# Second-norm operands stored by token parity, and DRAM weight sums paused while the decay rows load

## The chip, the cores and the metric

The kernel runs on one core of one Trainium2 chip. The metric is the time of one execution on the device, in microseconds. Before the change the median of three runs is 727.8 us (727.13 to 728.92). Engines are named as in the profile: PE is TensorE (its weight loads are shown apart, as PEld), DVE is VectorE, ACT is ScalarE, POOL is GpSimd, and SP is SyncE, which only issues DMAs here. A line such as L864 is a line of the kernel before the change.

## The reference

One layer of a decoder trunk on 512 tokens of width 1024, all in float32: a norm, one wide projection, two token mixers side by side (a block-sparse attention and a chunkwise mLSTM), their gated merge, an output projection with residual, a second norm, a SwiGLU feed-forward of width 2816 with residual, and a final norm.

```python
u = rms_norm(h, norm_mix_g)
z = u @ w_in                       # q/k/v | mLSTM q,k,v,o | gates
A = moba_attention(rope(q), rope(k), v)          # 8 heads x 64
B = mlstm_chunkwise(silu(conv(qk)), v, i, f)     # 4 heads x 128, per-row decay exp(b_t - b_s + i_s - m_t)
h = h + (sigmoid(ga) * (A @ w_proj_a) + sigmoid(gb) * (B_gated @ w_proj_b)) @ w_out
u = rms_norm(h, norm_ffn_g)
g, up = split(u @ w_gate_up)
h = h + (silu(g) * up) @ w_down
return rms_norm(h, norm_final_g)
```

## The kernel before, in words

**Products.** Every float32 product is made of three matmuls: the operands are split into a high and a low half (type fp32r), and high x high, high x low and low x high are summed in PSUM. `split_hl` (L164 to L169) makes the halves: ACT copies the high half, DVE subtracts it to give the low half.

**First stage, the units.** The projections are 60 units (`UNITS`, L53 to L71), each with one 512 KB block of weights and, in most, 24 matmuls of 128x512. `fill` (L376 to L394) runs the next unit `u`: it splits weights up to two units ahead, calls `make_sums` (L387), issues the unit's matmuls, and between these and the unit's evacuation runs a function `mid` that it is given. Weight blocks are loaded in pairs on SP's queue (L193) into nine rotating buffers (`NR`, tag R); a load is issued when a buffer is free.

**The mixer loop** (L1724 to L1763) runs steps `n`; each step from the second on runs one unit, and step n runs unit n + 9. Steps 0 to 15 are the attention's halves of heads, later steps are the mLSTM's. `mid` also starts side work that is listed by step in `todo` (L1720): `ml_w(h)` at steps 13, 16, 17 and 19. `ml_w` calls `ml_load` (L1604), which loads the decay rows of one mLSTM head, tile `R`, from a small DRAM array `scr`, broadcast to 128 partitions: one 896 KB DMA on POOL's queue. Then DVE (L1618) and ACT turn the rows into weights that multiply the mLSTM's scores. The tile comes from the pool of eight 4x512 tiles (tag A4), so the load also waits until such a tile is free.

**Sums in DRAM.** The feed-forward uses a Strassen-like scheme with seven products in place of eight, on halves of tokens and of widths. It needs sums of weight blocks. Some are made in DRAM ahead of time: `sum_steps` (L726) yields 40 steps, alternately a copy of one block to a DRAM tile `ws` (SP's queue, L730) and the addition of the other block (POOL's queue, an accumulating DMA, L732). The blocks have 1 MB (gate and up weights, `wgc`) or 512 KB (down weights, `wds`). `make_sums(n)` (L746) issues steps until n are made, and ties each to the newest matmul of the program so far, so that a step waits in its queue until PE is there ("paced"). `fill` asks for `6 * (u - 17) // 7` steps: the first at unit 19, then six in seven units. In the feed-forward each of the seven products of an item issues one more step (L855).

**Second norm's operands.** `run_wo` (L669 to L704) adds the output projection to the residual, feature block by feature block (`h`, 128 features x 512 tokens), and forms the scheme's seven left operands: `a` and `b` are the first and second 256 tokens of `h`; they are scaled by the norm's gain (L684, L685, L693, L694), combined by further DVE operations, split, and stored in tiles `bq` (`bpair`, `bop`). All of it is elementwise along the tokens.

**Feed-forward.** `ITEMS` (L85) lists the order: five items `gc` (512 columns of gate and up each) interleaved with four items `ds` (the matching rows of the down projection), then two items `gu` (the last 256 columns), then the last `ds`. In `gc_run` (L848) the tokens are the matmul's stationary side: for each product, `q = slice(t, HS, 2)` (L859) takes every second of the 256 tokens of a `bq` operand as a 128x128 stationary tile (t = 0 even, t = 1 odd tokens), and the 512 weight columns move. That makes 5 items x 7 products x 2 x 2 x 2 x 3 = 840 matmuls at L864 to L866. The outputs for t are transposed on DVE (L907) into a tile `ht` in which t is the innermost index, so token order is restored there. In `gu` items (`prod`, L1021) the weights are stationary and the `bq` operand moves, all 256 tokens; `gu_last` (L1075) applies the norm's row `rb2`, SiLU and the product, and splits the result `u` into `h` and `l` (L1093, L1094), which the last `ds` uses as stationary tiles by token. In `ds` the stationary tiles are contiguous (L1107 to L1109).

The order of the feed-forward's instructions comes from `plan` and `at` (L772 to L797), a table of due times by which the scheduler sorts each engine's queue.

Of the kernel before, what the change touches and what calls it, by code (L numbers as in the profile page):

```python
# [12 lines left out]
ALU = mybir.AluOpType  # L13
# [78 lines left out]
def hybrid_layer_kernel(ctx: ExitStack, tc, xT, wall, wgc, wgu, wds, wdl, g3v, vecs, wgates, consts, rope, out):  # L92
# [283 lines left out]
    def fill(n=1, mid=None):  # L376

        for _ in range(n):
            u = pos[0]
            if u >= len(UNITS):  # L380
                if mid:
                    mid()
                return
            while wstate["split"] <= min(u + LOOK, NGEN - 1):
                split_unit()
            pos[0] += 1
            make_sums(6 * (u - 17) // 7)  # L387
            kind, i = UNITS[u]
            g = run[kind](i, *whl.pop(u))
            next(g, None)  # L390
            if mid:
                mid()
            for _ in g:
                pass  # L394
# [7 lines left out]
        mm3(ps, wh, wl, range(8), uh, ul, True, True)  # L402
        return ps

    st = {"made": 0}

    def run_qk(kind):
        def fn(i, wh, wl):
# [241 lines left out]

    trq = []

    def residual():

        while trq:
            n, h = trq.pop(0)
            if n % 4 == 0:
                st["ht"] = slot4(name="ht").rearrange("p j (b e) -> p j b e", e=P)
            o = st["ht"].rearrange("p j b (n e) -> p (j b) n e", e=32)
            V.transpose(o[:, :, n % 4, :], h.rearrange("p (b e) -> p b e", e=32))  # L660
            if n % 4 == 3:
                c = 32 * (n - 3)
                for a in range(4):
                    nc.gpsimd.dma_start(
                        h1d[:, :, 256 * a + c : 256 * a + c + P].rearrange("t (b i) c -> i t b c", i=32),
                        st["ht"][32 * a : 32 * a + 32],
                    )

    def run_wo(i, wh, wl):  # L669
        if len(xr) < KT:  # L670
            load_xr()
        ps = mmb()
        mm3(ps, wh, wl, range(8), [t[0] for t in mgd], [t[1] for t in mgd], True, True)
        residual()
        yield
        m = i
        h = xr[WO.index(m)]
        V.tensor_tensor(h, ps, h, op=ALU.add)
        trq.append((WO.index(m), h))
        a, b = h[:, 0:HS], h[:, HS:S]  # L680
        g, ng = col(G2 + m), ng2[:, m : m + 1]
        if m < 4:
            u = ut[m] = slot(name="ut")
            V.tensor_scalar(u[:, 0:HS], a, g, None, op0=ALU.mult)  # L684
            V.scalar_tensor_tensor(u[:, HS:S], b, ng, u[:, 0:HS], op0=ALU.mult, op1=ALU.add)  # L685
            hh, ll = bpair(0, m)
            act_(hh, u, AF.Copy, scale=-1.0)
            V.scalar_tensor_tensor(ll, u, -1.0, f(hh), op0=ALU.mult, op1=ALU.subtract)
        else:
            k = m - 4  # L690
            u = ut.pop(k)
            v = slot(name="v1")
            V.tensor_scalar(v[:, 0:HS], a, g, None, op0=ALU.mult)  # L693
            V.tensor_scalar(v[:, HS:S], b, ng, None, op0=ALU.mult)  # L694
            split_hl(v, dst=bpair(1, k))
            w = slot(name="v2")
            V.tensor_tensor(w[:, 0:HS], u[:, HS:S], v[:, HS:S], op=ALU.subtract)
            V.tensor_tensor(w[:, HS:S], u[:, 0:HS], w[:, 0:HS], op=ALU.subtract)
            split_hl(w, dst=bpair(2, k))
            V.tensor_tensor(u[:, 0:HS], v[:, 0:HS], w[:, 0:HS], op=ALU.subtract)  # L700
            if k == 0:
                bq[(3, 0)] = slot4(F32R, "bq")
            split_hl(u[:, 0:HS], dst=bop(6, k))
        add_sq(2, h, WO.index(m))  # L704
# [41 lines left out]
    def make_sums(n):  # L746

        while st["made"] < n:
            st["made"] += 1
            i = next(making, None)  # L750
            if i is not None:
                tc.add_manual_dep(raw_ins(i), raw_ins(st["mm"]).name, after, reason="paced")
# [95 lines left out]
    def gc_run(c):  # L848

        key = ("gc", c)  # L850
        g = sw.pop(key)
        two = range(2)

        def product(ps, w, o, first=False):
            make_sums(st["made"] + 1)  # L855
            for j, (wh, wl) in enumerate(g[w]):
                for t in two:
                    at(key, w, 2720 * j + 1360 * t)
                    q = slice(t, HS, 2)  # L859
                    for e in range(2):  # L860
                        k = 2 * j + e
                        bh, bl = (b[:, q] for b in bop(o, k))
                        d = slice(e * S, (e + 1) * S)
                        st["mm"] = T.matmul(ps[t], bh, wh[:, d], start=first and k == 0, stop=False, skip_group_check=not first)  # L864
                        T.matmul(ps[t], bh, wl[:, d], start=False, stop=False, skip_group_check=not first)  # L865
                        T.matmul(ps[t], bl, wh[:, d], start=False, stop=k == 3, skip_group_check=not first)  # L866

        def done(w, t):
            at(key, w, 4080 + 1360 * t)

        def copies(ps, w, name):
            r = []
            for t in two:
                done(w, t)
                r.append(slot(name=name))
                act_(r[t], ps[t], AF.Copy)
            return r

        X = [mmb() for _ in two]
        product(X, "W11", 0, first=True)  # L880
        a = copies(X, "W11", "ga")
        Z = [sb() for _ in two]
        product(Z, "S1", 1, first=True)
        x3 = copies(Z, "S1", "gx")
        product(X, "S2", 4)
        b = copies(X, "S2", "gb")
        yield
        if c == 0:
            second_norm(key)
        rg = st["rg"]  # L890
        Y = [accb() for _ in two]
        product(Y, "W12", 2, first=True)
        for t in two:
            done("W12", t)
            V.tensor_tensor(a[t], Y[t], a[t], op=ALU.subtract)
        yield
        product(X, "S3", 5)
        for t in two:
            done("S3", t)
            V.tensor_tensor(x3[t], X[t], x3[t], op=ALU.add)  # L900
            act_(x3[t], x3[t], AF.Silu, scale=rg[:, t + 2 : t + 3])
        yield
        ht = slot4(name="ht").rearrange("p j (b h e x) -> p (j b) h e x", h=2, e=32, x=2)

        def turn(t, u, s):
            V.tensor_tensor(u, u, s, op=ALU.mult)
            V.transpose(ht[:, :, t // 2, :, t % 2], u.rearrange("p (b e) -> p b e", e=32))  # L907

        product(Z, "S4", 3)
        for t in two:  # L910
            done("S4", t)
            V.tensor_tensor(b[t], Z[t], b[t], op=ALU.add)
            at(key, "W22", 1360 * t)
            turn(t + 2, b[t], x3[t])
        product(X, "W22", 6)
        for t in two:
            done("W22", t)
            s = slot(name="gs")
            act_(s, X[t], AF.Silu, scale=rg[:, t : t + 1])
            turn(t, a[t], s)  # L920
        at(key, "W22", 5440 + 3000)
        d = hid_t[c] = dram.tile([P, 4, S], F32, name=nm("ad"))
        for i in range(4):
            nc.sync.dma_start(
                d[:, i].rearrange("(g o) x -> o g x", o=32), ht[32 * i : 32 * i + 32].rearrange("p (g b) h e x -> p g (b h e x)", g=4)
            )
# [148 lines left out]
    def gu_last(i):  # L1075
        key = ("gu", i)
        g = sw.pop(key)
        x, z, t, u, s12 = g["X"], g["Z"], g["t"], g["u"], g["s"]
        rb2 = st["rb2"]
        at(key, "S4")  # L1080
        prod(z, g["S4"], 3)
        at(key, "W22", E_OFF)
        V.scalar_tensor_tensor(u[:, B_], z, -1.0, s12[:, B_], op0=ALU.mult, op1=ALU.subtract)
        V.tensor_tensor(t[:, B_], t[:, B_], rb2[:, B_], op=ALU.mult)
        at(key, "W22")
        prod(x, g["W22"], 6)
        at(key, "W22", E_OFF + 1500)
        V.tensor_tensor(t[:, A_], x, rb2[:, A_], op=ALU.mult)
        act_(t, t, AF.Silu)
        V.tensor_tensor(u[:, A_], u[:, A_], t[:, A_], op=ALU.mult)  # L1090
        V.scalar_tensor_tensor(u[:, B_], u[:, B_], -1.0, t[:, B_], op0=ALU.mult, op1=ALU.mult)
        h, l = slot(F32R, "ach"), slot(F32R, "acl")
        c = act_(h, u, AF.Copy)  # L1093
        V.tensor_tensor(l, u, f(h), op=ALU.subtract)  # L1094
        hid.append((h, l))
        if i == FT - 1:
            ph["ins"].append(raw_ins(c))
# [626 lines left out]
    while n < len(steps) or qa or qb:  # L1724
# [14 lines left out]
        def mid():  # L1739
# [4 lines left out]
            advance(2 if n < 13 else 3)  # L1744
            second()

        if n:
            fill(1, mid)
        else:
            mid()  # L1750
# [126 lines left out]
```

## Time and profile before

| what | value |
|---|---|
| runs | 727.13, 727.8, 728.92 us; median 727.8 us |
| profiled execution, its own time | 727.12 us |
| its span, first to last instruction | 725.3 us |
| PE granted clock | 0.998 |
| busiest engines | PE 712.7 us, DVE 602.4 us, ACT 429.6 us, POOL 69.9 us |
| DMA | 152.70 MB, 211 GB/s on the mean |

The profile's page gives busy times by engine, the span in 40 slices, the DMA queues, the chain of work that ended last, and groups of instructions by source line. Its views of the trace give the same by stretches of time (windows), by instruction in order of time (timeline), by wait, and by tile. A timeline row has the start, the duration, the engine and line, the operation, out<-in, and in brackets the idle time before it with what ended it. A matmul's duration (0.39 us) is longer than the distance to the next matmul's start, since matmuls overlap in the array: what a matmul costs a busy PE is the distance from start to start.

### The profile page before, as it was taken

Reading aid. Unit: us, or ns where it says so; the run is one execution under the profiler, and the core shown is the slowest. Engines: PE = TensorE matmul, PEld = TensorE weight load, DVE = VectorE, ACT = ScalarE, POOL = GpSimd, SP = SyncE. Lnnn points to the kernel's source line nnn. Section 1 sums busy time; section 2 is a strip of 40 time slices with the busy share of each in tenths; the row PEclk is TensorE's granted clock in tenths of the full one; section 3 lists DMA queues with packets and bytes.
Section 4 is the critical chain, followed back from the end, with each engine's and each line's share of the span. In section 5 each row is a group of like instructions: output and inputs, shape, how many; then the busy total and the mean of one; then the engine's idle time right before and its main releaser. Section 6 shows DMA issues by size and latency. Waiting matters only on the chain.

```text
span 725.3 us, 9566 instructions
## 1 busy us (share of the span) xinstructions
PE 712.7 (98%) x3318; PEld 592.9 (82%) x3318; DVE 602.4 (83%) x982; ACT 429.6 (59%) x706; POOL 69.9 (10%) x97
## 2 busy tenths in 40 slices
PE   9999999999998999999999999999999999999995
PEld 6888788888887888888888888888888888888974
DVE  6799877898968588666699869898999789798996
ACT  7535777668754346723344746566665665575654
POOL 0013010001000000000020110021002004003000
PEclk9999999999999999999999999999999999999999
DMA  9668683676486456978889956479469649869703
GB/s 329 278 212 240 190 239 126 204 214 212 132 278 163 144 172 179 279 253 228 233 260 232 270 189 224 182 197 303 167 203 268 211 131 221 303 156 273 207 1 117
DMA packets 47008, 152.70 MB, mean 211 GB/s; under 512 B 5852, under 2 KB 6244, under 8 KB 42480
## 3 DMA queue, kind: packets, MB, share of 16 engines
q1 hardware_dynamic: 36880, 117.39, 47.3%
q0 software_dynamic: 9792, 34.14, 22.9%
q8 instruction: 26, 0.43, 0.2%
q10 hardware_dynamic: 288, 0.56, 0.2%
q14 instruction: 22, 0.18, 0.1%
HBM read 130.01 MB, written 53.52 MB: 253 GB/s over the span
## 4 chain that ended last, share of the span: by engine, by line
PE 91%; DVE 5%; DMA 2%; ACT 1%; issue 1%; ACTq 0%; DVEq 0%
PE mm L208 12%; PE mm L210 12%; PE mm L209 12%; PE mm L864 5%; PE mm L865 5%; PE mm L866 5%; PE s L864 3%; PE s L865 3%; PE s L866 3%; PE mm L1109 2%; PE mm L1108 2%; PE mm L1107 2%; PE acc L1587 2%; PE mm L491 2%; PE mm L308 2%; PE mm L493 2%
## 5 line engine op out<-in xcount | busy, mean ns | idle before, releaser
L155 ACT ACTIVATE w<-raw 128x1024 fp32r<-128x1024 f32 (+2 forms) x107 | 108.0, 1022 | 52.0 <-PE mm L865 16.2
L155 ACT ACTIVATE wh<-raw 128x1024 fp32r<-128x1024 f32 x56 | 59.1, 1056 | 74.6 <-PE mm L209 72.4
L839 DVE TENSOR_TENSOR w<-raw,w 128x1024 fp32r<-128x1024 f32 x70 | 84.1, 1220 | 18.4 <-ACT w L155 18.3
L168 DVE TENSOR_TENSOR wl<-raw,wh 128x1024 fp32r<-128x1024 f32 x56 | 68.2, 1219 | 9.2 <-ACT wh L155 8.9
L864 PE MATMUL mm<-w,bq 128*128 128x512 f32 x160 | 63.1, 394 | 0.0
L866 PE MATMUL mm<-w,bq 128*128 128x512 f32 x160 | 63.1, 394 | 0.0
L865 PE MATMUL mm<-w,bq 128*128 128x512 f32 x160 | 63.1, 394 | 0.0
L208 PE MATMUL mm<-u,wh 128*128 128x512 f32 x128 | 50.7, 396 | 2.7 <-DVE ga L587 2.5
L210 PE MATMUL mm<-u,wh 128*128 128x512 f32 x128 | 50.1, 391 | 0.0
L209 PE MATMUL mm<-u,wl 128*128 128x512 f32 x128 | 49.9, 390 | 0.0
L210 PE MATMUL mm<-ul,wh 128*128 128x512 f32 x128 | 49.8, 389 | 0.0
L208 PE MATMUL mm<-uh,wh 128*128 128x512 f32 x128 | 49.8, 389 | 0.0
L209 PE MATMUL mm<-uh,wl 128*128 128x512 f32 x128 | 49.8, 389 | 0.0
L864 PEld LDWEIGHTS mm<-w,bq 128*128 128x128 f32 x160 | 30.9, 193 | 6.5
L866 PEld LDWEIGHTS mm<-w,bq 128*128 128x128 f32 x160 | 30.9, 193 | 6.4
L865 PEld LDWEIGHTS mm<-w,bq 128*128 128x128 f32 x160 | 30.9, 193 | 6.4
L1019 DVE TENSOR_TENSOR w<-raw,w 128x1024 fp32r<-128x1024 f32 x25 | 30.2, 1219 | 2.7 <-ACT w L155 1.7
L864 PE MATMUL s<-w,bq 128*128 128x512 f32 x80 | 31.5, 394 | 0.0
L865 PE MATMUL s<-w,bq 128*128 128x512 f32 x80 | 31.5, 394 | 0.0
L866 PE MATMUL s<-w,bq 128*128 128x512 f32 x80 | 31.5, 394 | 0.0
L1107 PE MATMUL mm<-w,ac 128*128 128x512 f32 x80 | 31.4, 392 | 0.0
L1109 PE MATMUL mm<-w,ac 128*128 128x512 f32 x80 | 31.2, 390 | 0.0
(439 smaller groups left out, 1945.5 us busy)
## 6 DMA issues: line engine op xcount, KB each, us to landing
raw<-in_wall_dram SPq DMA_DIRECT2D x56, 512.0 KB, 5.7
raw<-in_wgc_dram SPq DMA_DIRECT2D x30, 512.0 KB, 6.0
raw<-ws SPq DMA_DIRECT2D x30, 512.0 KB, 5.7
ws<-in_wgc_dram SPq DMA_DIRECT2D x10, 1024.0 KB, 6.0
ws<-in_wgc_dram POOLq DMA_DIRECT2D x10, 1024.0 KB, 8.3
raw<-in_wds_dram SPq DMA_DIRECT2D x15, 512.0 KB, 6.1
ws<-in_wds_dram SPq DMA_DIRECT2D x10, 512.0 KB, 4.8
ws<-in_wds_dram POOLq DMA_DIRECT2D x10, 512.0 KB, 6.6
```

Source lines behind the costliest of these rows:

```text
L155: return A.activation(out_, in_, func, **kw)
L168: V.tensor_tensor(l, src, f(h), op=ALU.subtract)
L208: st["mm"] = T.matmul(ps, wh[:, c], rh[j], start=start and j == 0, stop=False)
L209: T.matmul(ps, wl[:, c], rh[j], start=False, stop=False)
L210: T.matmul(ps, wh[:, c], rl[j], start=False, stop=stop and j == n - 1)
L839: V.tensor_tensor(l, t, f(h), op=ALU.subtract)
L864: st["mm"] = T.matmul(ps[t], bh, wh[:, d], start=first and k == 0, stop=False, skip_group_check=not first)
L865: T.matmul(ps[t], bh, wl[:, d], start=False, stop=False, skip_group_check=not first)
L866: T.matmul(ps[t], bl, wh[:, d], start=False, stop=k == 3, skip_group_check=not first)
L1019: V.tensor_tensor(w[k][1], g[k], f(w[k][0]), op=ALU.subtract)
L1107: T.matmul(ps, bh, wh[:, d], start=first and k == 0, stop=False, skip_group_check=not first)
L1109: T.matmul(ps, bl, wh[:, d], start=False, stop=k == 1, skip_group_check=not first)
```

## The change

In four places:

- `gc_run` takes contiguous stationary tiles, `slice(t * P, (t + 1) * P)`. For that, `run_wo` stores the tokens of each operand half by parity: the even ones first, then the odd ones. It reads `h` through a view with stride two (`by_parity`) and writes through a view that is contiguous (`halves`).
- In `gu_last` the 256 tokens of each half are then in parity order too: the norm's row `rb2` is read with stride two, and the result's halves `h` and `l` are written with stride two, back in token order.
- `fill` asks for no new sum steps while `st["hold"]` is set, and otherwise for at most two more at a unit, up to the same schedule as before.
- The mixer loop sets `st["hold"]` in steps 12 to 20, that is for units 21 to 29.

```diff
@@ fill
-            make_sums(6 * (u - 17) // 7)
+            make_sums(st["made"] if st["hold"] else min(st["made"] + 2, 6 * (u - 17) // 7))
...
-    st = {"made": 0}
+    st = {"made": 0, "hold": False}
...
+    def by_parity(t):
+        return t.rearrange("p (j x) -> p x j", x=2)
+
+    def halves(t):
+        return (t[:, c].rearrange("p (x j) -> p x j", x=2) for c in (slice(0, HS), slice(HS, S)))
+
@@ run_wo
-        a, b = h[:, 0:HS], h[:, HS:S]
+        a, b = (by_parity(h[:, c]) for c in (slice(0, HS), slice(HS, S)))
         g, ng = col(G2 + m), ng2[:, m : m + 1]
         if m < 4:
             u = ut[m] = slot(name="ut")
-            V.tensor_scalar(u[:, 0:HS], a, g, None, op0=ALU.mult)
-            V.scalar_tensor_tensor(u[:, HS:S], b, ng, u[:, 0:HS], op0=ALU.mult, op1=ALU.add)
+            lo, hi = halves(u)
+            V.tensor_scalar(lo, a, g, None, op0=ALU.mult)
+            V.scalar_tensor_tensor(hi, b, ng, lo, op0=ALU.mult, op1=ALU.add)
...
             v = slot(name="v1")
-            V.tensor_scalar(v[:, 0:HS], a, g, None, op0=ALU.mult)
-            V.tensor_scalar(v[:, HS:S], b, ng, None, op0=ALU.mult)
+            lo, hi = halves(v)
+            V.tensor_scalar(lo, a, g, None, op0=ALU.mult)
+            V.tensor_scalar(hi, b, ng, None, op0=ALU.mult)
             split_hl(v, dst=bpair(1, k))
@@ gc_run
-                    q = slice(t, HS, 2)
+                    q = slice(t * P, (t + 1) * P)
@@ gu_last
-        V.tensor_tensor(t[:, B_], t[:, B_], rb2[:, B_], op=ALU.mult)
+        lo, hi = halves(t)
+        V.tensor_tensor(hi, hi, by_parity(rb2[:, B_]), op=ALU.mult)
...
-        V.tensor_tensor(t[:, A_], x, rb2[:, A_], op=ALU.mult)
+        V.tensor_tensor(lo, x.rearrange("p (x j) -> p x j", x=2), by_parity(rb2[:, A_]), op=ALU.mult)
...
         h, l = slot(F32R, "ach"), slot(F32R, "acl")
-        c = act_(h, u, AF.Copy)
-        V.tensor_tensor(l, u, f(h), op=ALU.subtract)
+        w, u = (lambda t: t.rearrange("p (s j x) -> p s x j", s=2, x=2)), u.rearrange("p (s x j) -> p s x j", s=2, x=2)
+        c = act_(w(h), u, AF.Copy)
+        V.tensor_tensor(w(l), u, w(f(h)), op=ALU.subtract)
@@ the mixer loop
+        st["hold"] = 12 <= n <= 20
         if n:
             fill(1, mid)
```

## The prediction

> **What bounds the kernel now.** I read the page first, for the share of each engine and for the chain of work that ended last.
>
> ```profile
> PE 712.7 (98%) x3318; PEld 592.9 (82%) x3318; DVE 602.4 (83%) x982; ACT 429.6 (59%) x706; POOL 69.9 (10%) x97
> PEclk9999999999999999999999999999999999999999
> PE 91%; DVE 5%; DMA 2%; ACT 1%; issue 1%; ACTq 0%; DVEq 0%
> ```
>
> PE is busy nearly all the time at full clock, and 91% of the chain is PE. So time is gained where a matmul costs PE less, or where PE stands still. Next the windows, to see where it does and how busy the others are there.
>
> ```profile
> 220.00:240.00 20.00, 17.52 (x86) 14.62 (x85) 14.85 (x25) 9.64 (x16) 0.83 (x1) 1.00 0.61 158
> 380.00:400.00 20.00, 20.00 (x89) 16.57 (x88) 19.07 (x33) 10.04 (x16) 0.83 (x1) 1.00 0.92 233
> 540.00:560.00 20.00, 20.00 (x88) 16.58 (x87) 19.65 (x20) 11.73 (x15) 6.94 (x8) 1.00 1.06 272
> 680.00:700.00 20.00, 19.48 (x108) 16.03 (x106) 19.08 (x30) 12.79 (x19) 0.00 (x0) 1.00 0.21 67
> ```
>
> The columns are PE, PEld, DVE, ACT, POOL, clock, DMA share and GB/s. The first row holds a hole of 2.5 us in PE. At 380 (output projection) and 540 (feed-forward) PE has no hole, though DVE is at 19.1 and 19.7 of 20. At 680 PE has small holes and DVE is full.
>
> **Contiguous stationary tiles.** The cost of a matmul is the distance of starts. These rows of PE's timeline are the first matmul of a unit of the output projection, the first of the first `gc` product 24 matmuls later, and the first of its second product, again 24 later; then the last matmul of a `gc` item and, 24 apart, two of the `ds` stage behind it, where the stationary tile is contiguous and weight columns move as in `gc`.
>
> ```profile
> 386.90 0.39 PE L208 MATMUL mm<-mgh,wh 128*128 128x512 f32 x1
> 392.34 0.39 PE L864 MATMUL mm<-w,bq 128*128 128x512 f32 x1
> 397.94 0.40 PE L864 MATMUL s<-w,bq 128*128 128x512 f32 x1
> ...
> 471.05 0.40 PE L866 MATMUL mm<-w,bq 128*128 128x512 f32 x1
> 471.28 0.39 PE L1107 MATMUL mm<-w,ac 128*128 128x512 f32 x1
> 476.73 0.39 PE L1107 MATMUL mm<-w,ac 128*128 128x512 f32 x1
> ```
>
> The output projection takes 5.44 us for 24, 226.7 ns each; `gc` 5.60, 233.3 ns; `ds` 5.45, 227.1 ns. The groups of weight loads show where it arises:
>
> ```profile
> L864 PEld LDWEIGHTS mm<-w,bq 128*128 128x128 f32 x160 | 30.9, 193 | 6.5
> L1107 PEld LDWEIGHTS mm<-w,ac 128*128 128x128 f32 x80 | 15.0, 188 | 3.6 <-DVE h L1191 0.4 <-issue 0.2
> ```
>
> A load with stride two takes 193 ns, a contiguous one 188. Type, size and moving operand are alike in both; the stride is the only difference that I find. The 840 matmuls of `gc` should fall from 233.3 to between 226.7 and 227.1 ns: 5.2 to 5.6 us, taken as 5.5. PE has no hole in `gc` to absorb it, if DVE keeps up: the full DVE at 540 did so, and 24 matmuls only bring a due time 0.16 us nearer.
>
> [...]
>
> **DVE and ACT with stride two.** In the output projection 12 DVE operations of 128x256 (L684, L685, L693, L694, four each) get a strided input. No row shows a strided read. The nearest is a strided write: L907 writes every second word of `ht`, L660 runs of 32.
>
> ```profile
> L907 DVE STREAM_TRANSPOSE ht<-ga 128x512 f32<-128x512 f32 x10 | 6.6, 690 | 0.0
> L660 DVE STREAM_TRANSPOSE ht<-xr 128x512 f32<-128x512 f32 x8 | 5.6, 703 | 0.0
> L168 DVE TENSOR_TENSOR bq<-v,bq 128x512 fp32r<-128x512 f32 x8 | 5.5, 684 | 0.0
> L168 DVE TENSOR_TENSOR bq<-ut,bq 128x256 fp32r<-128x256 f32 x4 | 1.7, 417 | 0.0
> ```
>
> It costs nothing there, which is the lower end; a gain I exclude, since nothing gets shorter. The upper end is an element that takes twice its time: 684 - 417 = 267 ns more per 256 elements, 12 x 0.27 = 3.2 us of DVE. What hides it is the lead of the operands. The last block before `gc`, and the weight halves that DVE makes beside it:
>
> ```profile
> 390.17 0.35 DVE L684 TENSOR_SCALAR ut<-xr,vec 128x256 f32<-128x256 f32 x1
> 393.15 0.69 DVE L688 SCALAR_TENSOR_TENSOR bq<-ut,bq 128x512 fp32r<-128x512 f32 x1
> 401.44 3.49 DVE L839 TENSOR_TENSOR w<-raw,w 128x1024 fp32r<-128x1024 f32 x3
> ```
>
> The first product needs this block (feature block 3) in its second half, 15 matmuls after 392.34, at 395.8; it is ready at 393.8, 2 us early, and two slower operations take at most 0.5. The three weight halves at 401.4 serve the third and fourth product, in the order of `GC_W`; the first is the second half of the third product's weights and ends at 402.6, and the matmul that reads it first, the 14th of that product, is due 61 matmuls after 392.34, at 406.6: 4 us of lead. So the output projection costs 0 at either end. If the lead were gone, it would be the 3.2 us.
>
> In `gu_last`, twice each, L1084 and L1088 read `rb2` strided, and ACT's copy and L1094 write strided (L1094 reads `h` strided too). DVE is the busy engine there, and the last stage's PE waits for just these results:
>
> ```profile
> 692.55 0.42 DVE L1088 TENSOR_TENSOR gt<-mm,rn 128x256 f32<-128x256 f32 x1
> 697.08 0.69 DVE L1094 TENSOR_TENSOR acl<-up,ach 128x512 fp32r<-128x512 f32 x1
> PEld acc L1225 <- ACT ach L155: 0.8, 1, 0.8
> PEld acc L1227 <- DVE acl L1094: 0.4, 1, 0.4
> ```
>
> By the free write of L907 this is 0; doubled, 2 x (0.27 + 0.27 + 0.53) = 2.1 us of DVE, and with an estimated 0.9 us for ACT's two copies 3 us in all. I take 0.2, near the row. [...]
>
> **The pause of the sums.** The hole at 222 is followed back along the chain, with POOL's and PE's timeline and the wait of DVE:
>
> ```profile
> 205.57 10.54 DMA R<-scr
> 216.75 0.61 DVE R L1618 x2
> 223.71 0.70 DVE ga L587
> 224.46 0.50 PE mm L208
> 203.99 0.83 POOL L732 DMA_DIRECT2D ws<-in_wgc_dram  x1 [14.20 <-PE mm L209]
> 205.57 0.56 POOL L1606 DMA_DIRECT2D R<-scr  x1 [0.75 <-PE acc L1587]
> 221.64 0.34 PE L1639 MATMUL mm<-qk 128*128 128x384 f32 x1
> DVE R L1618 <- DMA R<-scr: 4.9, 1, 4.9
> DMA to landing us min/median/max: 5.5/7.1/10.5
> ```
>
> The last decay rows (head 3) are issued at 205.57, when the attention frees their tile, and land after 10.5 us, the longest of the four; the median is 7.1, the least 5.5. A 1 MB sum went out 1.6 us before. DVE works in order, so it stands for 4.9 us, from 211.3 to 216.2, and the evacuation (L587) that frees PE's PSUM bank comes late: PE starts at 224.46 in place of 0.17 us after 221.64, a loss of 2.65 us.
>
> With the pause, steps 3 to 10 are not issued in units 21 to 29, and the sum at 203.99 is step 10. The issue at 205.57 stays, since a matmul releases it and not POOL's queue; the landing should come after 5.5 to 7.1 us, at 211.1 to 212.7. DVE then waits at most 1.4 us in place of 4.9, so L587 comes at least 3.5 us earlier, more than the 2.65. I take all 2.65; the lower end is 0, if the rows still land late. Next late would be DVE itself, at 14.85 of 20: nothing.
>
> What moves: eight steps slide past unit 29, and from unit 30 two come in each unit, until unit 36 has caught up with the schedule (16 steps). SP then has one copy a unit ahead of the weight blocks, POOL one addition, with nothing else on POOL until the residual's transposes. The weight blocks have nine buffers, so a block is issued about eight units of 5.44 us, some 43 us, ahead of its split, and is there 5.7 us later; ACT's splits wait for PE's buffers, not for the blocks:
>
> ```profile
> ACT wh L155 <- PE mm L209: 21.4, 6, 6.2
> raw<-in_wall_dram SPq DMA_DIRECT2D x56, 512.0 KB, 5.7
> q1 hardware_dynamic: 36880, 117.39, 47.3%
> q0 software_dynamic: 9792, 34.14, 22.9%
> ```
>
> That cover hides the crowd at no cost.
>
> **Sum.** 727.12 - 5.5 - 2.65 + 0.2 = 719.2 us for the profiled execution. It lies 0.7 under the median of the runs; taken off the median, the same sum gives 719.9. I name 719.5.
>
> **Rivals.**
>
> A, the forecast: 719.5.
>
> B, the rows still land late, or DVE finds PE another wait at the same place. For: the weight blocks that share DMA with them stay. Against: with such blocks about, the median of the four loads was 7.1 us. Then 719.5 + 2.65 = 722.2.
>
> C, strided operands cost about the doubled time in the tail, where DVE is full: 719.5 + 2.8 = 722.3. For: DVE at 19.08 of 20 and PE's two waits. Against: L907.
>
> D, the change doesn't do what it says: the strided tile is no slower, and `gc` is at 233 ns for something else in that stage, such as its DMA share of 1.06. Only the hole goes: 719.5 + 5.5 = 725.0. Against: `ds` runs at 227 from its first matmul on, 0.23 us behind the last of `gc` with the same transfers about, and the first `gc` product takes 233 at a share of 0.92. [...]
>
> E, slower: the caught-up sums crowd out the weight blocks. By q1 and q0 a MB costs all DMA engines 2.9 us (47.3% of 725.3 over 117.39) or 4.9 us. Three pairs of 1.05 MB, four of 0.52 MB and seven blocks take 51 us, against seven units of at least 38 us. The 13 us over are eaten by the lead of 37 us. It decides if crowded transfers cost over (38 + 37) / 51 = 1.5 times their mean; PE then waits. At the 1.9 times of the late rows (10.5 against 5.5) it is 97 - 75 = 22 us, 741 us. Against: at 540 DMA was at 1.06 and PE had no hole.
>
> **How the numbers follow.** Chances: A 0.66, B 0.12, C 0.11, D 0.06, E 0.05. The range reaches from 718.0 to 723.2. Its low end is the whole 5.6 with nothing lost in the tail, 718.9, less half the spread of the three runs, 0.9; its high end is B and C plus the same. A measurement can tell about 0.3%, 2.2 us, from no change, so faster means under 725.6. A, B, C and two thirds of D are faster: 0.93; the rest of D is the same: 0.02, and E's mild forms add 0.01; slower 0.04.
>
> **What would show it.** Right: in the profile after, 24 matmuls at L864 to L866 take 5.44 us and their weight loads 188 ns; the wait of L1618 for `R` is under 1.5 us; PE in 220 to 240 is at 20; L684 to L694 keep 350 to 460 ns. Wrong: weight loads at 188 but starts still 233 apart; DVE waiting for something else before L587; ACT's splits waiting for the weight blocks between 220 and 270; L1084, L1088 and L1094 longer than now, with more waits of PE before L1225.

## The result, and the profile after

The changed kernel takes 719.55 us (median of four runs, 719.12 to 720.01), beside 727.46 us (727.11 to 728.92) for the kernel before: a ratio of 0.9888, 95% interval 0.987 to 0.9905. The profiled execution took 719.12 us, its span is 717.3 us; before they were 727.12 and 725.3, so the two profiles differ by 8.0 us. Lines of `gc_run` from here on are those of the changed kernel: the product's matmuls are L872 to L874, `ds` has L1117 to L1119, the decay rows are loaded at L1616 and used at L1628, the sums are added at L740.

The engines, from the page:

```profile
PE 707.3 (99%) x3318; PEld 588.4 (82%) x3318; DVE 601.4 (84%) x982; ACT 428.9 (60%) x706; POOL 69.9 (10%) x97
```

PE's busy time is 5.4 us less, and the span 8.0: the rest, 2.6 us, was idle time. Three of the windows shown before, with the same columns (PE, PEld, DVE, ACT, POOL, clock, DMA share, GB/s):

```profile
220.00:240.00 20.00, 20.00 (x96) 16.88 (x96) 13.45 (x22) 7.10 (x12) 1.57 (x2) 1.00 0.94 268
540.00:560.00 20.00, 20.00 (x90) 16.57 (x89) 16.38 (x15) 12.07 (x15) 3.47 (x4) 1.00 1.02 268
680.00:700.00 20.00, 19.44 (x94) 15.69 (x94) 19.15 (x29) 10.92 (x16) 0.00 (x0) 1.00 0.00 1
```

The hole at 222 is gone. Where it was, DMA is now at 0.94 instead of 0.61: the sums that were held back run here, and PE does not notice. In the feed-forward at 540, 90 matmuls fall in these 20 us, and 88 did before. The window at 680 holds other work than before, since the kernel is some 8 us ahead there; 19.44 against 19.48 says only that small holes are left, such as PE's wait for `ach`, 0.47 us at 688.17 and 0.43 at 696.10 before.

PE's timeline, for the distances of starts:

```profile
389.39 0.39 PE L872 MATMUL mm<-w,bq 128*128 128x512 f32 x1
394.83 0.39 PE L872 MATMUL s<-w,bq 128*128 128x512 f32 x1
...
466.31 0.39 PE L874 MATMUL mm<-w,bq 128*128 128x512 f32 x1
466.53 0.39 PE L1117 MATMUL mm<-w,ac 128*128 128x512 f32 x1
...
469.25 0.39 PE L1117 MATMUL s<-w,ac 128*128 128x512 f32 x1
```

The first `gc` product now takes 5.44 us for its 24 matmuls, 226.7 ns each, as the output projection did before. Twelve of `ds` take 2.72 us, the same pitch. The rows also place the gain: the first `gc` matmul came at 392.34 and comes 2.95 us earlier; the last one of the `gc` item before this `ds` came at 471.05 and comes 4.74 us earlier; the end is 8.0 us earlier. So 2.95 us were won before the feed-forward, and the other 5 us grow along it, in `gc` alone: matched one by one, the 420 matmuls of `ds` keep their distances within 0.2 us in sum. A group of weight loads in `gc`:

```profile
L872 PEld LDWEIGHTS mm<-w,bq 128*128 128x128 f32 x160 | 30.0, 188 | 6.7 <-ACT gs L160 0.5
```

It takes 188 ns, as in `ds`. Next, the decay rows: the timelines of POOL, DVE and PE around the last head's load, and then the tile's own summary of the four loads.

```profile
205.15 0.53 POOL L1616 DMA_DIRECT2D R<-scr  x1 [35.72 <-PE acc L1597]
217.43 0.89 POOL L740 DMA_DIRECT2D ws<-in_wgc_dram  x1 [11.75 <-DMA ws<-in_wgc_dram]
210.98 1.12 DVE L1628 SCALAR_TENSOR_TENSOR R<-con,cS,R 128x128 f32<-128x128 f32 x4
220.15 0.69 DVE L587 TENSOR_TENSOR ga<-mm,rn 128x512 f32<-128x512 f32 x1
221.40 0.34 PE L1649 MATMUL mm<-qk 128*128 128x384 f32 x1
221.57 0.40 PE L208 MATMUL mm<-u,wh 128*128 128x512 f32 x1
```

```profile
DMA to landing us min/median/max: 4.3/5.3/6.8
```

The load is issued at nearly the same moment as before (205.15 for 205.57, of which 0.24 is an earlier start of the whole), still released by the attention's matmul, but no sum goes out ahead of it; the next one follows at 217.43. DVE reaches the rows at 210.98 and waits for nothing (a bracket would show it). The evacuation at L587, which came at 223.71, comes at 220.15, ahead of PE's need, and PE goes on 0.17 us after L1649. Compared by the instruction, PE's L208 moved from 224.46 to 221.57: 2.65 us of hole, and 0.24 of an earlier start of the first matmuls, which has nothing to do with the change.

How the sum held up the rows is seen in what the DMA queues carried from 205.6 to 210.6, right behind the load's issue. Queue q0 is the one on which POOL's sums and rows go, q1 that of SP's loads; before, then after:

```profile
DMA packets 108, 0.88 MB, mean 177 GB/s; under 512 B 0, under 2 KB 0, under 8 KB 0
q0 software_dynamic: 108, 0.88, 96.6%
```

```profile
q0 software_dynamic: 144, 0.92, 47.8%
```

The rows are 896 KB on 128 partitions, 7 KB each. Before, no packet is under 8 KB, so none of these is theirs: for five us the sum had the DMA engines to itself, and the rows did not share with it but stood behind it. After, the 0.92 MB of q0 are the rows.

### The profile page after: what moved, and what is told of

The parts are those of the page before. It is cut to its first block, busy times and chain, and to the rows that moved or that the text cites. A ratio compares the mean times of both kernels' runs of the same rounds, so it can differ in the third digit from the quotient of the medians.

```text
span 717.3 us, 9566 instructions
## 1 busy us (share of the span) xinstructions
PE 707.3 (99%) x3318; PEld 588.4 (82%) x3318; DVE 601.4 (84%) x982; ACT 428.9 (60%) x706; POOL 69.9 (10%) x97
## 4 chain that ended last, share of the span: by engine, by line
PE 84%; DVE 7%; ACT 5%; DMA 2%; issue 1%; POOL 0%; ACTq 0%; DVEq 0%; POOLq 0%
PE mm L208 10%; PE mm L209 10%; PE mm L210 10%; PE mm L872 5%; PE mm L873 5%; PE mm L874 5%; PE s L873 2%; PE s L874 2%; PE s L872 2%; PE mm L1118 2%; PE mm L1119 2%; PE mm L1117 2%; PE mm L491 2%; PE mm L308 2%; PE mm L493 2%; PE mm L492 2%
## 5 line engine op out<-in xcount | busy, mean ns | idle before, releaser
L168 DVE TENSOR_TENSOR wl<-raw,wh 128x1024 fp32r<-128x1024 f32 x56 | 68.2, 1219 | 10.5 <-ACT wh L155 10.0
L872 PE MATMUL mm<-w,bq 128*128 128x512 f32 x160 | 62.4, 390 | 0.0
L874 PE MATMUL mm<-w,bq 128*128 128x512 f32 x160 | 62.3, 389 | 0.0
L873 PE MATMUL mm<-w,bq 128*128 128x512 f32 x160 | 62.2, 389 | 0.0
L208 PE MATMUL mm<-u,wh 128*128 128x512 f32 x128 | 50.6, 395 | 0.2 <-ACT ob L155 0.2
L208 PE MATMUL mm<-uh,wh 128*128 128x512 f32 x128 | 49.8, 389 | 0.0
L872 PEld LDWEIGHTS mm<-w,bq 128*128 128x128 f32 x160 | 30.0, 188 | 6.7 <-ACT gs L160 0.5
L873 PEld LDWEIGHTS mm<-w,bq 128*128 128x128 f32 x160 | 30.1, 188 | 6.2
L874 PEld LDWEIGHTS mm<-w,bq 128*128 128x128 f32 x160 | 30.0, 188 | 6.2
L1117 PE MATMUL mm<-w,ac 128*128 128x512 f32 x80 | 31.3, 392 | 0.0
L1118 PE MATMUL mm<-w,ac 128*128 128x512 f32 x80 | 31.1, 389 | 0.0
L1119 PE MATMUL mm<-w,ac 128*128 128x512 f32 x80 | 31.1, 389 | 0.0
L872 PE MATMUL s<-w,bq 128*128 128x512 f32 x80 | 31.1, 389 | 0.0
L873 PE MATMUL s<-w,bq 128*128 128x512 f32 x80 | 31.1, 389 | 0.0
## 6 DMA issues: line engine op xcount, KB each, us to landing
ws<-in_wgc_dram POOLq DMA_DIRECT2D x10, 1024.0 KB, 10.1
```

The lines of the kernel that those rows point to most:

```text
L168: V.tensor_tensor(l, src, f(h), op=ALU.subtract)
L208: st["mm"] = T.matmul(ps, wh[:, c], rh[j], start=start and j == 0, stop=False)
L1117: T.matmul(ps, bh, wh[:, d], start=first and k == 0, stop=False, skip_group_check=not first)
L1118: T.matmul(ps, bh, wl[:, d], start=False, stop=False, skip_group_check=not first)
L1119: T.matmul(ps, bl, wh[:, d], start=False, stop=k == 1, skip_group_check=not first)
```

## The experiments

Two causes were claimed: the stride of the stationary tiles in `gc` (5.5 us), and one DMA that meets another (2.65 us). The rivals were that `gc` is slow for another reason, that the rows are late for another reason, that strided VectorE reads take it back, and that the delayed sums crowd the weight blocks. The first four kernels were measured side by side; the kernel before had 727.4 us there.

**The parity layout without the pause.**

```diff
-            make_sums(st["made"] if st["hold"] else min(st["made"] + 2, 6 * (u - 17) // 7))
+            make_sums(6 * (u - 17) // 7)
```

> The parity layout alone: the weight sums are issued by the old rule, without the pause. Theory (two independent gains that add): the hole of 2.65 us on TensorE near 222 us comes back, whole, and the shorter weight loads of the gc units stay, so the time is 719.5 + 2.65 = 722.2 us, within 0.4. Rival 1 (the earlier, not the shorter, work of the gc stage is the gain, so that the pause is needed for all of it): about 727 us. Rival 2 (the hole was closed by something else than the pause): 719.5 us.

Measured: median 724.33 us (721.04 to 727.63 over nine runs), ratio 0.9945 [0.9921, 0.997]. The profiled execution is as expected: 722.26 us, loads of 188 ns in `gc`, and the hole is back. Its chain of waits, and the window in which the hole ends:

```profile
205.51 10.74 DMA R<-scr
223.84 0.70 DVE ga L587
224.58 0.50 PE mm L208
```

```profile
224.00:226.00 2.00, 1.42 (x6) 1.18 (x7) 2.00 (x3) 0.00 (x0) 0.00 (x0) 1.00 0.98 193
```

Rows after 10.74 us, L208 at 224.58. But the median lies 2.1 us above the expected time, and the runs spread over 6.6 us, where the same layout with a pause spreads over about 1. The mean granted clock of these runs goes from 0.997 in the shortest to 0.992 in the longest. None of the rivals says that. In the medians the two gains do not simply add: 3.1 us for the layout alone, 2.9 for the pause alone (next run), 8.1 for both (the run after it). The run with the doubled transfer, below, was made for it.

**The pause without the parity layout**, the kernel before with the lines on `st["hold"]`.

> The pause alone, with the old layout of tokens in the second-norm operands. Theory: the hole of 2.65 us goes, the stationary tiles of the gc units keep their stride of two and their 233 ns per matmul, so 727.5 - 2.65 = 724.8 us, within 0.4; weight loads of the gc product take 193 ns. Rival 1 (the gc pitch of 227 ns comes from less DMA traffic or an earlier start, not from the layout): 719.5 us and 188 ns loads. Rival 2 (the later sums cost something in the first gc unit that only the faster gc units repay): 725.5 us or more.

Measured: 724.46 us (724.13 to 725.28), ratio 0.9953 [0.9936, 0.9969]. The theory holds, and rival 1 falls: with the same pause and the same sums, the strided layout keeps its loads of 193 ns in all three groups, one of which is

```profile
L864 PEld LDWEIGHTS mm<-w,bq 128*128 128x128 f32 x160 | 30.9, 193 | 6.5
```

**The pause for one step only.**

```diff
-        st["hold"] = 12 <= n <= 20
+        st["hold"] = n == 20
```

> The change, but the pause lasts for one step of the mixer only, the one ahead of the last head's decay rows, so that just the sum added at 204 us waits. Theory (one 1 MB transfer shares the DMA engines with the rows of the last head, and it alone makes the hole): 719.5 us, within 0.4, the rows land in 5 to 7 us. Rival (the backlog of the sums before it also loads the queues, so that the long pause is needed): part or all of the 2.65 us comes back, 720.5 to 722.2 us, and the rows take 8 us or more.

Measured: 719.33 us (719.2 to 720.03), ratio 0.988 [0.9855, 0.9906], and the four loads of rows:

```profile
DMA to landing us min/median/max: 4.3/6.0/7.0
```

One sum made the hole. The other seven steps that the change delays could have stayed where they were. Between this kernel and the one with the pause alone lie the layout and the length of the pause: 724.46 - 719.33 = 5.1 us. The change itself, with the long pause, took 719.55 and, repeated below, 719.77 beside other runs, which makes the layout worth 4.7 to 5.1 us.

**The stride put into another stage.**

```diff
@@ ds_prod
-        c = slice(t * P, (t + 1) * P)
+        c = slice(t, 2 * P, 2)
```

> The change, and in addition the ds units read their stationary tile with a stride of two, every second column of the same 256 instead of 128 neighbours; the output rows come out in another order of tokens, the amount of work is the same. Theory (a stride of two costs a matmul 6.6 ns wherever its path is TensorE-bound): 420 matmuls x 6.6 ns = 2.8 us, 722.3 us, within 0.5, and weight loads of 193 ns in place of 188 ns. Rival 1 (the 6.6 ns belonged to the gc operands, their buffers or writers, not to the stride): 719.5 us. Rival 2 (ds is paced by its weight splits and hides it): 719.5 to 720.5 us with 193 ns loads.

Measured: 721.66 us (721.48 to 721.96), ratio 0.9911 [0.9883, 0.9939]; 2.3 us more than the run above it, a little under the 2.8 expected. A group of `ds` loads, and PE's timeline:

```profile
L1117 PEld LDWEIGHTS mm<-w,ac 128*128 128x128 f32 x80 | 15.5, 193 | 3.5 <-DVE h L1201 0.3
```

```profile
466.91 0.39 PE L1117 MATMUL mm<-w,ac 128*128 128x512 f32 x1
...
469.71 0.39 PE L1117 MATMUL s<-w,ac 128*128 128x512 f32 x1
```

Twelve matmuls take 2.80 us, 233.3 ns each: the loss went with the stride, out of `gc` and into `ds`. That settles the first cause, by experiment and not by likeness.

**How the price goes with the stride.** Two kernels read the operand's words further apart.

```diff
@@ gc_run, product (at a stride of four; at eight: 2 * z + t and 8)
-                        bh, bl = (b[:, q] for b in bop(o, k))
+                        src = bq[(min(o // 2, 3), (k // 2) * (o < 6))].rearrange("p x c -> p (x c)")
+                        at0 = 1024 * (k % 2)
+                        bh, bl = (src[:, at0 + 512 * z + t : at0 + 512 * z + t + 4 * P - 3 : 4] for z in (0, 1))
```

> The change, but each stationary tile of the gc product takes every fourth word of its operand buffer instead of 128 neighbours (the words belong to other tokens, so the values are wrong; the number and shape of matmuls are the same). Theory A (the cost of a stride grows in steps of the spread: 188 ns loads at one, 193 at two): 840 loads of some 203 ns if it grows with the spread, a pitch of 240 ns or less, time up to 730 us. [...] Theory C (there is one price for any stride): 193 ns loads, 725 us.

> As the run with a stride of four, with every eighth word (values wrong, same matmuls). Theory A (grows with the spread): loads of 220 ns or more and a pitch that then follows the load, 255 ns or so, time 745 us. [...] Theory C (one price for any stride): 193 ns loads, 725 us.

Measured at four: 726.26 us (ratio 0.997 [0.9949, 0.9991]); at eight: 733.63 us (1.0071 [1.0051, 1.0091]). A group of loads and 24 matmuls of the first product, at four and then at eight (the product's lines are L874 to L876 here):

```profile
L874 PEld LDWEIGHTS mm<-w,bq 128*128 128x128 f32 x160 | 49.5, 309 | 0.2
```

```profile
389.92 0.40 PE L874 MATMUL mm<-w,bq 128*128 128x512 f32 x1
395.56 0.40 PE L874 MATMUL s<-w,bq 128*128 128x512 f32 x1
```

```profile
L874 PEld LDWEIGHTS mm<-w,bq 128*128 128x128 f32 x160 | 52.8, 330 | 0.2
```

```profile
389.51 0.41 PE L874 MATMUL mm<-w,bq 128*128 128x512 f32 x1
395.39 0.41 PE L874 MATMUL s<-w,bq 128*128 128x512 f32 x1
```

| stride of the stationary tile | load, ns | pitch of the matmuls, ns |
|---|---|---|
| 1 | 188 | 226.7 |
| 2 | 193 | 233.3 |
| 4 | 309 | 235.0 |
| 8 | 330 | 245.0 |

The loads jump between two and four, from 193 to 309 ns, and the pitch does not follow: a load of 309 ns is longer than the pitch of 235.0 and still costs only 8.3 ns more of it than a contiguous one. So in these traces loads lie over each other as well as over matmuls (the idle column says 0.2), and the duration of a load does not tell its price. Eight costs 10.0 ns a matmul more than four; theory A has the growth but not the jump; C falls. What sets the pitch between 233 and 245 stays open.

**The same stride on the moving side.** One kernel takes every second weight column, another takes pairs of neighbours and skips the next pair.

```diff
@@ first kernel
-                        d = slice(e * S, (e + 1) * S)
+                        d = slice(e, 2 * S, 2)
@@ second kernel, in place of wh[:, d] and wl[:, d]
+                        wh2, wl2 = (y.rearrange("p (j y x) -> p j y x", y=2, x=2)[:, :, e, :] for y in (wh, wl))
```

> The change, but the moving operand of the gc product takes every second of 1024 weight columns instead of 512 neighbours (values wrong, same matmuls; the stationary tiles stay contiguous). Theory (the loss at a stride of two belongs to the load of the stationary tile, where 128 words come in one after another; 512 moving columns have their own pace): pitch 227 ns, 719.5 us, loads 188 ns. Rival (any strided read by TensorE loses in proportion to its columns, 5 ns for 128, so 20 ns for 512): pitch some 247 ns, 840 x 20 ns = 17 us, 736 us.

> The change, but the moving operand of the gc product takes pairs of neighbouring words and skips the next pair (256 x 2 words out of 1024; values wrong, same matmuls). At a plain stride of two, as many words of each 16 bytes, the pitch went from 227 to 452 ns. Theory A (two words enter TensorE at a time, and only neighbours can): 227 ns, some 720 us. Theory B (what counts is how many bytes the moving columns span): 452 ns as at the plain stride, 909 us.

Measured: 908.96 us (ratio 1.2486 [1.2417, 1.2554]) and 909.03 us (1.2495 [1.2452, 1.2538]). PE's timeline, 24 matmuls of each:

```profile
390.25 0.61 PE L872 MATMUL mm<-w,bq 128*128 128x512 f32 x1
401.11 0.64 PE L872 MATMUL s<-w,bq 128*128 128x512 f32 x1
```

```profile
389.66 0.61 PE L872 MATMUL mm<-w,bq 128*128 128x512 f32 x1
400.51 0.64 PE L872 MATMUL s<-w,bq 128*128 128x512 f32 x1
```

10.86 and 10.85 us, 452 ns each: twice 226. Theory and rival of the first kernel are both wrong: the moving side is not free, and its price is no few ns but the whole matmul again, 840 x 226 ns = 190 us. The pairs leave theory B of the second kernel standing, in which neighbours alone don't help; why it is just a factor of two was not found.

**VectorE at a stride of eight.**

```diff
-        a, b = (by_parity(h[:, c]) for c in (slice(0, HS), slice(HS, S)))
+        a, b = (by_parity(h[:, c], 8) for c in (slice(0, HS), slice(HS, S)))
```

(`by_parity` and `halves` take the stride as an argument.)

> The change, but the second-norm multiplications of the output projection read every eighth token instead of every second (the halves of the transform then hold other tokens, so the values are wrong; the operations and their sizes are the same). Theory (VectorE's strided reads are free here): tensor_scalar 350 ns and scalar_tensor_tensor 462 ns as before, 719.5 us. [...]

Measured: 720.16 us (ratio 0.9892 [0.9838, 0.9947]). The groups, in the changed kernel and then here:

```profile
L691 DVE TENSOR_SCALAR ut<-xr,vec 128x256 f32<-128x256 f32 x4 | 1.4, 352 | 0.0
L692 DVE SCALAR_TENSOR_TENSOR ut<-xr,ng,ut 128x256 f32<-128x256 f32 x4 | 1.8, 462 | 0.0
```

```profile
L691 DVE TENSOR_SCALAR ut<-xr,vec 128x256 f32<-128x256 f32 x4 | 1.9, 464 | 0.0
L692 DVE SCALAR_TENSOR_TENSOR ut<-xr,ng,ut 128x256 f32<-128x256 f32 x4 | 2.7, 682 | 0.0
```

Two is free (352 and 462 ns, for 349 and 461 before the change) and eight is not: 112 and 220 ns more. So the theory falls at eight in the durations, though hardly in the time: by these two rows the sixteen such operations (the two tensor_scalars of each later block like L691's) are 4 x (3 x 0.112 + 0.220) = 2.2 us of VectorE, of which little shows in 720.16 us, for the 719.5 expected.

**The transfer doubled**, without a pause and with one more copy of 1 MB at that point.

```diff
+            make_sums(6 * (u - 17) // 7)
+            if st["hold"]:
+                x = nc.sync.dma_start(dram.tile(list(wgc[0, 3].shape), F32, name=nm("xx")), wgc[0, 3], max_dma_last_dim=8192)
+                tc.add_manual_dep(raw_ins(x), raw_ins(st["mm"]).name, after, reason="paced")
...
+        st["hold"] = n == 20
```

> The parity layout with the old rule for the sums, and one more copy of 1 MB from DRAM to DRAM (its result is not used) issued together with the sum that meets the decay rows of the last head. Theory (the rows are late because they share the DMA engines): alone they took 4.3 us, beside one transfer 10.7; beside two some 16 us, so TensorE's hole grows from 2.8 to some 8 us and the time from 722.3 to 727.5 us or more. Rival 1 (one transfer fills the share that they can lose): rows still 10 to 11 us, 722.3 us. Rival 2 (a longer hole also lowers the clock granted after it, as the runs with a mean clock of 0.992 were the longest with the old rule): more than the hole, 729 us or more, and a granted clock below 1.00 in the windows behind it.

Measured: 727.24 us (725.74 to 728.42), ratio 0.9993 [0.9978, 1.0008]. Chain, timeline and windows:

```profile
205.69 13.33 DMA R<-scr
```

```profile
227.36 0.79 PE L208 MATMUL mm<-u,wh 128*128 128x512 f32 x1 [5.28 <-DVE ga L590]
228.80 0.63 PE L208 MATMUL mm<-u,wh 128*128 128x512 f32 x1
229.23 0.63 PE L209 MATMUL mm<-u,wl 128*128 128x512 f32 x1
```

```profile
226.00:228.00 2.00, 0.64 (x2) 0.55 (x3) 1.97 (x3) 0.63 (x1) 0.00 (x0) 0.76 1.02 193
228.00:230.00 2.00, 2.00 (x6) 1.60 (x5) 2.00 (x4) 0.00 (x0) 0.00 (x0) 0.50 1.04 213
230.00:232.00 2.00, 2.00 (x9) 1.58 (x8) 0.57 (x2) 0.00 (x0) 0.00 (x0) 0.89 0.80 258
```

The rows take 13.3 us, between one transfer's 10.7 and the 16 expected. The copy, on SP's queue, runs beside the sum and slows it: the sum lands 11.5 us after its issue, for 8.9 without the copy, and the rows come behind it. Whether rows on a queue of their own would also get in beside the sum, no run here tests. PE's wait is 5.28 us and not the expected 8, so the time stays under the 727.5 us of the theory and the 729 of rival 2. But rival 2 has its sign: behind that hole the granted clock is 0.50, the matmuls start 0.43 us apart, and only after 230 are they back at 0.23. So this hole of 5.28 us cost its length and then some 1.5 us at half clock (six matmuls from 227.95 on lose 0.2 us each, the ones around them the rest); the hole of 2.67 us in the parity layout alone left the clock at 1.00. Where between these two holes the clock begins to fall, no run here shows.

**The next small wait.** In the profile after there is one new stall: at 429.24 PE takes 0.44 us from one start to the next and then 0.34, 0.3 us over its pitch, behind ScalarE, which waits for a column of the second norm.

```profile
425.82 1.34 ACT L160 ACTIVATE gx<-gx,rg 128x512 f32<-128x512 f32 x2 [4.84 <-DMA rg<-row]
429.24 0.39 PE L874 MATMUL mm<-w,bq 128*128 128x512 f32 x1
429.68 0.50 PE L872 MATMUL mm<-w,bq 128*128 128x512 f32 x1
```

The pause was cut to one step, and this column was read first:

```diff
-        columns(rb2[0:1, :], rc.rearrange("p (j h) -> p j h", h=1))
-        V.tensor_scalar(nrc, rc, -1.0, None, op0=ALU.mult)
         ...
         nc.gpsimd.dma_start(rg.rearrange("p (h x) -> p h x", x=2), d[0].rearrange("(h p x) -> p h x", h=2, x=2))
+        nc.gpsimd.dma_start(rc, d[0].rearrange("(j p) -> p j", p=P))
+        V.tensor_scalar(nrc, rc, -1.0, None, op0=ALU.mult)
```

> The change itself once more, beside the runs of this group: 719.5 us.

> The change with the pause of one step, and the second norm's column for the gate read first, from one shared row in DRAM instead of a row of its own behind the other column. Theory (in the changed kernel TensorE waits 0.32 us at 429 us behind the ScalarE activation that this column holds up): the column lands about 1 us earlier, the wait goes, 719.2 us. Rival (the next late thing, ScalarE's splits of the weight blocks or the other column on VectorE, takes its place): 719.5 us.

Measured: the change again 719.77 us (719.49 to 720.3), ratio 0.9895 [0.9872, 0.9917]; with the column first 719.4 us (719.03 to 719.85), 0.9888 [0.9867, 0.9908]. The difference is within the runs. In the repeated change the stall is nearly gone:

```profile
426.25 1.34 ACT L160 ACTIVATE gx<-gx,rg 128x512 f32<-128x512 f32 x2 [4.58 <-DVE nrc L991]
429.93 0.39 PE L874 MATMUL mm<-w,bq 128*128 128x512 f32 x1
430.45 0.40 PE L873 MATMUL mm<-w,bq 128*128 128x512 f32 x1
```

Two starts take 0.52 us, 0.06 over the pitch. By the clock `gx` comes later here, but PE is later still: `gx` starts 3.68 us ahead of the matmul before the stall, and 3.42 ahead in the first profile. Other traces lie on the same line: 3.59 us ahead and 0.15 of stall with the column first, 3.47 and 0.27 with the pause of one step, 2.98 and 0.77 with the transfer doubled; lead and stall add up to 3.74 to 3.76 us in all eight traces that have contiguous tiles in `gc`. In the four with strided ones the lead is 4.0 us or more, and there is no stall. So the stall is no accident of one execution: it is what the shorter pitch lays bare, at a size that goes with the moment at which the column arrives. The edit did not bring `gx` clearly sooner, and bought nothing that can be told.

## Why the prediction was right, point by point

**Contiguous stationary tiles: 5.5 us taken.** Right in cause and size. The pitch fell to 226.7 ns, the loads to 188 ns, layout against layout with a pause gives 4.7 to 5.1 us, and the stride moved to `ds` took its 233.3 ns along. Rival D, 233 ns for another reason, is excluded. The loads' durations and the pitch do not go together: from one to two the loads grew by 5 ns (188 to 193) and the pitch by 6.6, from two to four the loads by 116 ns (to 309) and the pitch by 1.7.

**DVE and ACT with stride two: 0.2 us taken.** In the output projection 0 was right: 352 and 462 ns against 349 and 461 before. The working miscounted, though: four lines with four operations each are sixteen and not twelve, so the upper end should have been 4.3 us and not 3.2; at a price of 0 it made no difference. In the tail DVE's operations kept their time, and ScalarE's strided copy became a little longer:

```profile
L155 ACT ACTIVATE ach<-up 128x512 fp32r<-128x512 f32 x2 | 1.3, 654 | 0.0
L1104 DVE TENSOR_TENSOR acl<-up,ach 128x512 fp32r<-128x512 f32 x2 | 1.4, 682 | 0.0
```

The copy took 617 ns and takes 654, twice: 0.07 us (the 0.9 us that the prediction put at its upper end for ACT was worked out from no row), and PE's weight loads of the last stage wait 0.9 us for `ach` in place of 0.8. Rival C fell. The reads, free at a stride of two, are not at eight: there 256 elements took 112 ns more in one operation and 220 in the other, or 0.43 and 0.86 ns each.

**The pause: 2.65 us taken whole.** Right, and for the reason given: the sum issued 1.6 us ahead holds up the rows, as the pause of one step shows. The last head's rows landed after 4.3 us, sooner than the expected 5.5 to 7.1; DVE's wait, at most 1.4 us in the prediction, is none. In the medians the pause is worth more than that: 2.9 us with the old layout, 5.0 with the new one. The step that was too narrow is that the hole was sized from one execution. Side by side, the runs spread over about 1 us with a pause, and without one over 6.6 (new layout) and 5.7 (old), so what the pause removes varies from execution to execution. After the 5.28 us hole of the doubled transfer the clock's half rate (0.50) came on top; that this is what spread the runs without a pause is likely from their clocks (0.997 in the shortest of the new layout, 0.992 in the longest), but only the doubled transfer has a trace of it. One step of a pause would have done, which the prediction did not see, though it had named that one sum.

**What moves: hidden.** Right. The crowd is there:

```profile
raw<-in_wall_dram SPq DMA_DIRECT2D x56, 512.0 KB, 5.5
ws<-in_wgc_dram POOLq DMA_DIRECT2D x10, 1024.0 KB, 10.1
```

The sums themselves land later than before (10.1 us for 8.3 in the additions of 1 MB), the weight blocks at their median don't (5.5 for 5.7), and PE has its full 20 us from 220 on. Rival E's condition, 1.5 times the mean for every transfer, was not met.

**The sum.** 719.2 us was expected of the profiled execution, and it took 719.12. Its terms: 2.65 for the hole, 5.1 to 5.5 for the stride, 0.24 from an earlier start that nobody asked for, less 0.3 of the stall at 429, for which the prediction had no term (it asked whether DVE keeps up with a faster `gc`, and not whether the column does), and under 0.1 in the tail where 0.2 was taken. The hit to a tenth is partly luck; the two large terms are not.

## What to carry to other kernels

- Keep both operands of a matmul contiguous in the order in which TensorE reads them: here a stride of two words cost 3% on the stationary side (233.3 for 226.7 ns a matmul) and a factor of two on the moving side (452 ns), and moving a permutation of tokens into VectorE's reads, at a stride of two, was free (352 and 462 ns for 349 and 461).
- When one engine stands still for a DMA that is at times twice as late, look for what was issued just before it and shift that one transfer, not a whole train. Here the late rows stood in line behind a larger transfer: 10.5 us to their landing, and 4.3 without it.
- Price a hole by more than its length: here one of 2.7 us left the clock whole, and one of 5.3 us was followed by some 1.5 us lost at half clock. Side by side, the runs without the pause also spread over 6.6 us (new layout) and 5.7 (old), those with it over about 1.
- When a stage gets faster, look for what now arrives too late for it: here a lead of 4 us shrank under 3.75, and part of the gain went into a wait that was not there before.

## What the hardware showed that was not expected

- A stationary load of 309 ns (stride of four) sustained a pitch of 235 ns: the duration of a load was no bound on the pitch here.
- A moving operand with a stride of two words, or in pairs of words with a gap of a pair, doubled the pitch from 226.7 to 452 ns; the loads beside it took 207 instead of 188 ns.
- The 896 KB of decay rows landed 4.3 us after their issue with no sum about, 10.7 behind one of 1 MB, and 13.3 when one more copy of 1 MB slowed that sum (11.5 us to its landing, for 8.9).
